# Recurrent branch of a hybrid decoder layer: the gate's sigmoid from exp and tanh instead of a reciprocal, and the low parts of two groups of weights made on VectorE

## The chip, the cores and the metric

The kernel runs on one core of one Trainium2 chip. The metric is the device time of one execution in microseconds (us), lower is better. Engines are named as the profile names them: PE is TensorE (PEld its weight loads), DVE is VectorE, ACT is ScalarE, POOL is GpSimd and SP is SyncE, whose queue issues nearly all transfers.

## The reference

One layer works on 2048 tokens of width 1024 in float32. A normed input goes through one wide projection, whose columns feed three branches: attention with a forgetting bias, a chunked state-space branch (SSD), and a gated linear recurrence over 512 channels. The branch outputs are gated, joined and projected back. The change is in the recurrence:

```
def rglru_mixer(x_raw, conv_w, conv_b, w_a, b_a, w_x, b_x, lam):
    xc = causal_dwconv(x_raw, conv_w, conv_b)
    xb = xc.reshape(bsz, seq, LRU_BLOCKS, LRU_BLOCK_DIM)
    r = sigmoid(einsum('bsnd,nde->bsne', xb, w_a) + b_a)
    i = sigmoid(einsum('bsnd,nde->bsne', xb, w_x) + b_x)
    log_a = -8.0 * r * softplus(-lam)
    a = exp(log_a)
    mult = where(first token, 1.0, sqrt(-expm1(2.0 * log_a)))
    b = mult * (i * xc)
    h[t] = a[t] * h[t-1] + b[t]          # an associative scan
y_lru = rglru_mixer(...) * silu(z_lru)
```

## The kernel before

Each float32 matrix is split into a high and a low part, and a product is three matmuls (high x high, high x low, low x high). `weights` (L172) does this for one group of columns of the input projection: for each of 8 row blocks k it loads `wr` (L184), ACT casts it to the high part `wh` (L186), and an engine that the caller picks (`eng`) subtracts to make the low part `wl` (L187). There are four raw buffers `wr` and nine pairs `wh`, `wl`; so of a new group only row block 0 can be made early, and block k needs the pair that the old group's block k-1 leaves when PE has used it for the last time.

The stages of the program are written one after the other: norm and transposes; the SSD inputs; one group for attention values; then the recurrent stage; then the gate path of the SSD (`zs`, L586 to L597) with the small decay computation `gates`; the SSD units and the attention projections; attention with a first output sweep; and a second output sweep. The order of each engine's queue is set by a scheduler when the program is built, and each engine runs its queue strictly in order.

The recurrent stage (L493 to L582) loops over four blocks m of 128 channels. A block has four pieces of 512 tokens (tb), and each piece three steps, run in the order `LORD`: `x` (projection `pll` on PE, conv on ACT and DVE), `z` (projection `pzl`, gate silu with two POOL multiplications into `ZZ`, L533 to L535), and `g`. On PE a block is 8 projections of 24 matmuls and 4 gate steps of 6, so 216 matmuls. Steps g2 and g3 come last; on ACT, DVE and POOL they run while PE works on the next group, whose weights must be ready by then. Step `g` (L539) computes both gates (`pgal` and `pgxl` in two PSUM buffers), the decay and its square root; after every second piece (one half block, hb, of 1024 tokens) it takes a square root on ACT (L570, with a table load), multiplies (L573), runs the scan on DVE (L574), multiplies into `ZZ` (L578) and stores it to `lr_d` (L579). `ZZ` has one buffer, so the copies L533 of the next half wait until that store has landed, and PE in turn waits for the PSUM that these copies free.

The lines that the change touches in step `g` are, for the recurrence gate r:

```
                pg = gate("a")
                A.activation(ra[:, sl], pg, AF.Exp, scale=-1.0, bias=c1("ba", m))
                V.tensor_scalar(ra[:, sl], ra[:, sl], 1.0, 3.0e38, op0=ALU.add, op1=ALU.min)
                V.reciprocal(ra[:, sl], ra[:, sl])
```

The low parts `wl` of the four recurrent groups and of the first two `zs` groups, 48 in all, are made on POOL; those of all other groups on DVE.

Of the kernel before, what the change touches and what calls it, by code (L numbers as in the profile page):

```python
# [12 lines left out]
AF = mybir.ActivationFunctionType  # L13
ALU = mybir.AluOpType
# [4 lines left out]
P = 128  # L19
# [25 lines left out]
def hybrid_block(ctx, tc, x, norm_g, w_in, q_norm_g, k_norm_g, forget_b, ssd_conv_w, ssd_conv_b,  # L45
# [37 lines left out]
    def ctile(name, shape, dt=F32):  # L83
        return cp.tile(shape, dt, name=name, tag=name)
# [13 lines left out]
    cv = ctile("cv", [P, NV])  # L98
# [4 lines left out]
    dt = ctile("dt", [P, NT, 16])  # L103
    etot = ctile("etot", [P, NT, 16])
    rsn = ctile("rsn", [P, NT, 2])
    lsp = ctile("lsp", [P, 4])
    nlsp = ctile("nlsp", [P, 4])


    def rsqrt(pool, y, v, n, tag):  # L110
# [83 lines left out]
    with tpool(name="p0", bufs=2) as p0, tpool(name="p01", bufs=1) as p01, \  # L194
# [44 lines left out]
        def c1(name, i=0):  # L239
            j = CV[name] + i  # L240
            return cv[:, j:j + 1]
# [24 lines left out]
        for tb in range(4):  # L266
            if tb + AHEAD < 4:
                norm_x(tb + AHEAD)
            for k in range(KD):
                pt, tag = ((psY, "Y"), (pst, "pt"))[(tb * KD + k) % 5 % 2]  # L270
                pt = pt.tile([P, 512], F32, name=f"pu{tb}_{k}", tag=tag)
                for i in range(4):
                    T.transpose(pt[:, i * P:(i + 1) * P],
                                xts[tb * 4 + i][:, k * P:(k + 1) * P], ident)
                g = ngc[:, k:k + 1]
                A.activation(uh[tb][k], pt, AF.Copy, scale=g)
                V.scalar_tensor_tensor(ul[tb][k], pt, g, uh[tb][k].bitcast(F32),
                                       op0=ALU.mult, op1=ALU.subtract)
            if tb == 0:
                pr = psY.tile([P, P], F32, name="pr2", tag="Y")  # L280
                T.transpose(pr, rows, ident)
                V.tensor_copy(cv, pr[:, 0:NV])


                j = CV["cw"]
                V.tensor_scalar(cv[:, j:j + 60], cv[:, j:j + 60], 0.5, None, op0=ALU.mult)
                j = CV["qg"]
                V.tensor_scalar(cv[:, j:j + 1], cv[:, j:j + 1], 0.125, None, op0=ALU.mult)
                j = CV["ba"]
                V.tensor_scalar(cv[:, j:j + 4], cv[:, j:j + 4], -1.0, None, op0=ALU.mult)  # L290
                j = CV["bx"]
                V.tensor_scalar(cv[:, j:j + 4], cv[:, j:j + 4], 0.5, None, op0=ALU.mult)

# [85 lines left out]
    with tpool(name="cvp", bufs=2) as pool, tpool(name="cl", bufs=1) as cl:  # L379
        for gq in range(6):  # L380
            if gq == 3:
                ll = cl.tile([P, 4], F32, name="ll")
                j = CV["lam"]
                V.tensor_scalar(ll, cv[:, j:j + 4], -1.0, None, op0=ALU.mult)
                softplus(cl, lsp, ll, [P, 4], "spl")
                V.tensor_scalar(lsp, lsp, 8.0, None, op0=ALU.mult)
                V.tensor_scalar(nlsp, lsp, -1.0, None, op0=ALU.mult)
            w = weights([(C_X + gq * 256, 256)]) if gq else wx0
            prev = [None, None]
            for tb in range(4):  # L390
                for mm in range(2):
                    m = gq * 2 + mm
                    nm = f"x{m}_{tb}"
                    ps = proj_ch(w, mm, tb, f"px{nm}")
                    acc = pool.tile([P, 512], F32, name=f"acc{nm}", tag="acc")
                    prev[mm] = conv(pool, ps, prev[mm], "cw", "cb", m, nm, 12, acc, str(mm), rtp)
                    th = pool.tile([P, 512], F32, name=f"thx{nm}", tag="thx")
                    A.activation(th, acc, AF.Tanh)
                    V.scalar_tensor_tensor(acc, th, 1.0, acc, op0=ALU.add, op1=ALU.mult)
                    ts = slice(tb * 512, tb * 512 + 512)  # L400
                    if m >= 8:
                        dma((bt_d if m < 10 else ct_d)[m % 2][:, ts], acc)
                    if m < 10:
                        pt = pst.tile([P, 4, P], F32, name=f"ptx{nm}", tag="pt")
                        for i in range(4):
                            T.transpose(pt[:, i, :], acc[:, i * P:(i + 1) * P], ident)
                        st = pool.tile([P, 4, P], F32, name=f"st{nm}", tag="stx")
                        A.copy(st, pt)
                        if m < 8:
                            dst = xs_d[m // 4][ts, (m % 4) * P:(m % 4 + 1) * P]  # L410
                        else:
                            dst = b_d[m - 8][ts, :]
                        dma(dst.rearrange("(i p) c -> p i c", p=P), st)
# [76 lines left out]
    with tpool(name="lxs", bufs=2) as lxs, tpool(name="lp1", bufs=1) as lp1, tpool(name="lp", bufs=2) as pool:  # L490
        wbd = {}
        HB = 1024
        for m in range(4):  # L493
            w = weights([(C_XL + m * P, P), (C_ZL + m * P, P)], eng=G)
            prev = [None]
            for nm, src in (("a", lru_w_a), ("x", lru_w_x)):
                wh = lp1.tile([P, P], F32R, name=f"bdh{nm}{m}", tag=f"bdh{nm}")
# [41 lines left out]
            def stage_g(tb):  # L539
                hb, sl, nm = part(tb)  # L540
                if tb % 2 == 0:
                    RA[hb] = pool.tile([P, HB], F32, name=f"RA{m}_{hb}", tag="RA")
                    MM[hb] = lp1.tile([P, HB], F32, name=f"MM{m}_{hb}", tag="MM")
                xc, ra, mm, zz = XC[hb], RA[hb], MM[hb], ZZ[hb]
                xh, xl = xp.pop(tb)

                def gate(k):
                    wh, wl = wbd[k, m]
                    pg = pst.tile([P, 512], F32, name=f"pg{k}{nm}", tag="pt")
                    T.matmul(pg, wh, xh, start=True, stop=False)  # L550
                    T.matmul(pg, wl, xh, start=False, stop=False)
                    T.matmul(pg, wh, xl, start=False, stop=True)
                    return pg

                pg = gate("a")
                A.activation(ra[:, sl], pg, AF.Exp, scale=-1.0, bias=c1("ba", m))
                V.tensor_scalar(ra[:, sl], ra[:, sl], 1.0, 3.0e38, op0=ALU.add, op1=ALU.min)
                V.reciprocal(ra[:, sl], ra[:, sl])
                pg = gate("x")
                t1 = pool.tile([P, 512], F32, name=f"ti{nm}", tag="t1")  # L560
                A.activation(t1, pg, AF.Tanh, scale=0.5, bias=c1("bx", m))
                V.scalar_tensor_tensor(xc[:, sl], t1, 1.0, xc[:, sl], op0=ALU.add, op1=ALU.mult)
                t2 = pool.tile([P, 512], F32, name=f"tt{nm}", tag="t1")
                A.activation(t2, ra[:, sl], AF.Tanh, scale=lsp[:, m:m + 1])
                A.activation(ra[:, sl], ra[:, sl], AF.Exp, scale=nlsp[:, m:m + 1])
                A.activation(mm[:, sl], ra[:, sl], AF.Square)
                V.scalar_tensor_tensor(mm[:, sl], mm[:, sl], 1.0, t2, op0=ALU.add, op1=ALU.mult)
                if tb % 2 == 0:
                    return
                A.activation(mm, mm, AF.Sqrt)  # L570
                if hb == 0:
                    V.memset(mm[:, 0:1], 1.0)
                V.tensor_tensor(xc, xc, mm, op=ALU.mult)  # L573
                V.tensor_tensor_scan(mm, ra, xc, 0.0 if hcol[0] is None else hcol[0],  # L574
                                     op0=ALU.mult, op1=ALU.add)
                hcol[0] = lp1.tile([P, 1], F32, name=f"hc{m}_{hb}", tag="hc")
                V.tensor_copy(hcol[0], mm[:, HB - 1:HB])
                V.scalar_tensor_tensor(zz, mm, 0.25, zz, op0=ALU.mult, op1=ALU.mult)  # L578
                dma(lr_d[m][:, hb * HB:(hb + 1) * HB], zz)  # L579
# [5 lines left out]
    with tpool(name="zp", bufs=2, side="right") as pool, tpool(name="g1", bufs=1, side="right") as g1:  # L585
        for gq in range(4):  # L586
            if gq == GM:
                gates(g1)
            w = weights([(C_ZS + gq * 256, 256)], eng=G if gq < 2 else V)
            for t2 in range(8):  # L590
                zt = pool.tile([P, 2, 256], F32, name=f"zs{gq}_{t2}", tag="zs")
                ps = proj_tok2(w, t2, f"pzs{gq}_{t2}", (pst, "pt") if t2 % 5 > 2 and gq == 0 else None)
                th = pool.tile([P, 2, 256], F32, name=f"thzs{gq}_{t2}", tag="thzs")
                A.activation(th, ps, AF.Tanh, scale=0.5)
                V.scalar_tensor_tensor(zt, th, 1.0, ps, op0=ALU.add, op1=ALU.mult)
                dst = zs_d[gq // 2][t2 * 256:(t2 + 1) * 256, (gq % 2) * 256:(gq % 2 + 1) * 256]
                dma(dst.rearrange("(i p) c -> p i c", p=P), zt)  # L597
# [455 lines left out]
```

## Time and profile before

| | |
|---|---|
| median of 3 runs | 2083.0 us (2082.02 to 2092.18) |
| profiled execution | 2094.4 us, of which the span from first to last instruction is 2092.4 us |
| PE busy | 2011.2 us, 96% of the span |
| DVE busy | 1278.1 us, 61% |
| ACT busy | 954.3 us, 46% |
| POOL busy | 542.0 us, 26% |
| mean granted TensorE clock | 0.985 of full speed |
| recurrent stage on PE | 376 to 582 us after the start |

The profile is one execution. Where PE is busy without a gap nothing that other engines do shows in the time; so what counts are the gaps of PE, and the stretches in which its clock was granted below full speed.

### The profile page before, as it was taken

What the parts mean: (1) busy time and instruction counts of PE and PEld (TensorE: products, weight loads), DVE (VectorE), ACT (ScalarE), POOL (GpSimd) and SP (SyncE); (2) the same over time, 40 slices, a digit from 0 to 9 for tenths busy, and PEclk for the clock granted to TensorE, in tenths of its full rate; (3) what the DMA queues carried; (4) which work ended last, traced back from release to release, by engine and by line L of the source; (5) the groups of instructions that cost most, each with busy time, mean ns of one, the idle gap of its engine ahead of it and who ended that gap; (6) DMA issues with size and microseconds to landing.
All of it is one profiled execution on the core that took longest, in us unless ns stands there. A gap on an engine that the chain in (4) does not pass through costs nothing. (4 is left out here: it accounts for less than half of the span.)

```text
span 2092.4 us, 38943 instructions
## 1 busy us (share of the span) xinstructions
PE 2011.2 (96%) x14021; PEld 1838.4 (88%) x14021; DVE 1278.1 (61%) x2844; ACT 954.3 (46%) x1985; POOL 542.0 (26%) x750
## 2 busy tenths in 40 slices
PE   7999999999999999998999998999999999998999
PEld 6788888887789998887888996989999999997999
DVE  6654555488874226767576245677787787774333
ACT  8444443466642215454444234566556565652100
POOL 0000001355531004454552001342233323121110
PEclk9999999999999999999999999999999999998999
DMA  5122233111123225666655636365435535234443
GB/s 195 41 71 61 71 112 93 42 42 42 42 72 98 82 80 165 188 182 197 190 166 177 167 116 205 100 165 144 116 110 147 132 105 155 64 100 139 137 133 106
DMA packets 277826, 248.59 MB, mean 119 GB/s; under 512 B 58725, under 2 KB 225153, under 8 KB 275585
## 3 DMA queue, kind: packets, MB, share of 16 engines
q1 hardware_dynamic: 277472, 246.07, 40.6%
q8 instruction: 111, 1.82, 0.4%
q0 software_dynamic: 160, 0.03, 0.1%
q14 instruction: 83, 0.67, 0.1%
HBM read 159.83 MB, written 86.18 MB: 118 GB/s over the span
## 5 line engine op out<-in xcount | busy, mean ns | idle before, releaser
L977 PE MATMUL po<-woh,mh 128*128 128x256 f32 x1024 | 295.2, 289 | 7.3 <-ACT mh L956 7.3
L981 PE MATMUL po<-woh,ml 128*128 128x256 f32 x1024 | 289.3, 283 | 0.0
L979 PE MATMUL po<-wol,mh 128*128 128x256 f32 x1024 | 288.2, 282 | 0.0
L876 ACT CAST ph<-T 128x512 fp32r<-128x512 f32 (+2 forms) x352 | 163.4, 490 | 144.4 <-PE T L869 79.7
L877 DVE TENSOR_TENSOR pl<-T,ph 128x512 fp32r<-128x512 f32 (+2 forms) x352 | 191.0, 563 | 32.5 <-ACT ph L876 32.2
L977 PEld LDWEIGHTS po<-woh,mh 128*128 128x128 f32 x1024 | 193.8, 189 | 10.4 <-ACT mh L956 8.0
L979 PEld LDWEIGHTS po<-wol,mh 128*128 128x128 f32 x1024 | 194.4, 190 | 2.7
L981 PEld LDWEIGHTS po<-woh,ml 128*128 128x128 f32 x1024 | 193.4, 189 | 1.0
L820 ACT ACTIVATE L<-L,mx 128x1920 f32<-128x1920 f32 (+15 forms) x128 | 154.7, 1209 | 54.6 <-DVE mx L819 39.0
L869 PE MATMUL T<-ident,L 128*128 128x128 f32 x1088 | 175.6, 276 | 1.2 <-ACT L L820 0.8
L373 DVE SCALAR_TENSOR_TENSOR accx<-rtx,cv,accx 128x512 f32<-128x512 f32 x144 | 104.6, 752 | 90.4 <-ACT accx L370 76.2
L855 PE MATMUL O<-ph,vv 128*128 128x256 f32 x576 | 154.7, 288 | 3.0 <-ACT ph L876 3.0
L322 PE MATMUL pxx<-uh,wh 128*128 128x512 f32 x384 | 152.7, 400 | 4.7 <-ACT rtx L365 3.3
L856 PE MATMUL O<-pl,vv 128*128 128x256 f32 x576 | 154.1, 291 | 1.0 <-DVE pl L877 0.9
L323 PE MATMUL pxx<-ul,wh 128*128 128x512 f32 x384 | 153.4, 400 | 0.0
L313 PE MATMUL pqk<-wl,uh 128*128 128x256 f32 x512 | 152.6, 299 | 0.8 <-DVE wl L187 0.8
L324 PE MATMUL pxx<-uh,wl 128*128 128x512 f32 x384 | 152.3, 398 | 0.0
L312 PE MATMUL pqk<-wh,uh 128*128 128x256 f32 x512 | 147.8, 293 | 3.0 <-ACT wh L186 3.0
L809 POOL TENSOR_SCALAR_AFFINE_SELECT cm<-cb 128x384 f32<-128x384 f32 (+3 forms) x128 | 58.7, 460 | 352.8 <-DVE mx L816 229.9
L314 PE MATMUL pqk<-wh,ul 128*128 128x256 f32 x512 | 149.5, 294 | 0.0
L313 PE MATMUL pzs<-wl,uh 128*128 128x256 f32 x512 | 144.5, 284 | 3.2 <-POOL wl L187 3.2
L314 PE MATMUL pzs<-wh,ul 128*128 128x256 f32 x512 | 144.4, 283 | 0.0
(313 smaller groups left out, 5661.2 us busy)
## 6 DMA issues: line engine op xcount, KB each, us to landing
ab<-acs_d SPq DMA_DIRECT2D x64, 256.0 KB
wr<-in_w_in_dram SPq DMA_DIRECT2D x192, 64.0 KB
wr<-in_w_in_dram SPq DMA_DIRECT2D x80, 128.0 KB
xt<-in_x_dram SPq DMA_DIRECT2D x16, 512.0 KB
xs_d<-stx SPq DMA_DIRECT2D x32, 256.0 KB
v_d<-vs SPq DMA_DIRECT2D x32, 256.0 KB
zs_d<-zs SPq DMA_DIRECT2D x32, 256.0 KB
xs<-xs_d SPq DMA_DIRECT2D x32, 256.0 KB
```

The source lines that it names most:

```text
L313: T.matmul(ps[:, i, :], h[k][:, sl], wl[k], start=False, stop=False)
L314: T.matmul(ps[:, i, :], l[k][:, sl], wh[k], start=False, stop=(k == KD - 1))
L323: T.matmul(ps, wh[k][:, ms], ul[tb][k], start=False, stop=False)
L820: A.activation(lt[:, 0:n], lt[:, 0:n], AF.Exp, bias=mx, accum_out=sm[:, i:i + 1])
L855: T.matmul(po[:, ca], vv[:, kt, :], ph[:, jj, ca], start=(kt == 0), stop=False)
L856: T.matmul(po[:, ca], vv[:, kt, :], pl[:, jj, ca], start=False, stop=(kt == nk - 1))
L869: ins = T.transpose(pt[:, jj, i * P:(i + 1) * P], L[i][:, kt * P:(kt + 1) * P], ident)
L876: A.copy(ph[:, ja, ca], pt[:, ja, ca])
L877: V.tensor_tensor(pl[:, ja, ca], pt[:, ja, ca], ph[:, ja, ca].bitcast(F32), op=ALU.subtract)
L977: T.matmul(o, mh[:, j, :], h[:, cs], start=(j == 0), stop=False, skip_group_check=True)
L979: T.matmul(o, mh[:, j, :], l[:, cs], start=False, stop=False, skip_group_check=True)
L981: T.matmul(o, ml[:, j, :], h[:, cs], start=False, stop=(j % 4 == 3), skip_group_check=True)
```

## The change

For the recurrence gate, sigmoid(z) = 1/(1 + exp(-z)) is replaced by exp(min(z, 0)) (1 + tanh(|z|/2)) / 2. The factor 2 that is left goes into the constant `lsp` (4 in place of 8). For each of the 16 pieces ACT had one exp and DVE an add with a clamp and a reciprocal; now ACT has a tanh from PSUM and an exp, and DVE a min that reads PSUM, an absolute value and a product. The gate's PSUM buffer is now read by two engines. The 48 low parts that POOL made are made by DVE, since `weights` is called without `eng`. Two more small instructions prepare the constants.

```diff
@@ constants
-    lsp = ctile("lsp", [P, 4])
-    nlsp = ctile("nlsp", [P, 4])
+    lpar = ctile("lpar", [P, 12])
+    lsp, nlsp, bab = (lpar[:, i * 4:i * 4 + 4] for i in range(3))
...
-                V.tensor_scalar(cv[:, j:j + 4], cv[:, j:j + 4], -1.0, None, op0=ALU.mult)
+                V.tensor_copy(bab, cv[:, j:j + 4])
+                V.tensor_scalar(cv[:, j:j + 4], cv[:, j:j + 4], 0.5, None, op0=ALU.mult)
...
-                V.tensor_scalar(lsp, lsp, 8.0, None, op0=ALU.mult)
+                V.tensor_scalar(lsp, lsp, 4.0, None, op0=ALU.mult)
@@ recurrent stage
-            w = weights([(C_XL + m * P, P), (C_ZL + m * P, P)], eng=G)
+            w = weights([(C_XL + m * P, P), (C_ZL + m * P, P)])
...
                 pg = gate("a")
-                A.activation(ra[:, sl], pg, AF.Exp, scale=-1.0, bias=c1("ba", m))
-                V.tensor_scalar(ra[:, sl], ra[:, sl], 1.0, 3.0e38, op0=ALU.add, op1=ALU.min)
-                V.reciprocal(ra[:, sl], ra[:, sl])
+                A.activation(ra[:, sl], pg, AF.Tanh, scale=0.5, bias=c1("ba", m))
+                V.tensor_scalar(mm[:, sl], pg, bab[:, m:m + 1], 0.0, op0=ALU.add, op1=ALU.min)
+                A.activation(mm[:, sl], mm[:, sl], AF.Exp)
+                V.scalar_tensor_tensor(ra[:, sl], ra[:, sl], -1.0, ra[:, sl], op0=ALU.mult,
+                                       op1=ALU.max)
+                V.scalar_tensor_tensor(ra[:, sl], ra[:, sl], 1.0, mm[:, sl], op0=ALU.add,
+                                       op1=ALU.mult)
@@ gate path of the SSD
-            w = weights([(C_ZS + gq * 256, 256)], eng=G if gq < 2 else V)
+            w = weights([(C_ZS + gq * 256, 256)])
```

The queues move with it. The first place is DVE at the end of recurrent block 2 (names: `XC` the conv result, `RA` the gate and decay, `MM` the root and the scan's result, `hc` its last column). Before, from the product ahead of the scan to the first gate step after it:

```order
L573 TENSOR_TENSOR XC_0_4603<-XC_0_4603,MM_0_4708 128x1024
L574 SCALAR_TENSOR_TENSOR MM_0_4708<-RA_0_4707,XC_0_4603 128x1024
L577 COPY hc_0_4818<-MM_0_4708 128x1
L578 SCALAR_TENSOR_TENSOR ZZ_0_4676<-MM_0_4708,ZZ_0_4676 128x1024
L557 TENSOR_SCALAR RA_1_4919<-RA_1_4919 128x512
L558 RECIPROCAL RA_1_4919<-RA_1_4919 128x512
```

The same place on DVE now, where lines after L558 have moved (the scan is L580, the product into `ZZ` L584, the min L559, the absolute value L561):

```order
L579 TENSOR_TENSOR XC_0_4619<-XC_0_4619,MM_0_4724 128x1024
L374 SCALAR_TENSOR_TENSOR XC_1_4746<-rtl_3_4867,cv,XC_1_4746 128x512
L580 SCALAR_TENSOR_TENSOR MM_0_4724<-RA_0_4723,XC_0_4619 128x1024
L187 TENSOR_TENSOR wl_1_4999<-wr_1_4997,wh_1_4998 128x256
L583 COPY hc_0_4838<-MM_0_4724 128x1
L584 SCALAR_TENSOR_TENSOR ZZ_0_4692<-MM_0_4724,ZZ_0_4692 128x1024
L187 TENSOR_TENSOR wl_2_5006<-wr_2_5004,wh_2_5005 128x256
L187 TENSOR_TENSOR wl_3_5013<-wr_3_5011,wh_3_5012 128x256
L187 TENSOR_TENSOR wl_4_5020<-wr_4_5018,wh_4_5019 128x256
L187 TENSOR_TENSOR wl_5_5027<-wr_5_5025,wh_5_5026 128x256
L559 TENSOR_SCALAR MM_1_4940<-pgal_2_4941,lpar 128x512
L561 SCALAR_TENSOR_TENSOR RA_1_4939<-RA_1_4939 128x512
```

A last conv step has come ahead of the scan; the next group's low part 1 stands right behind the scan, parts 2 to 5 behind the product into `ZZ`, and the min that frees the gate's PSUM buffer behind part 5.

The second place is ACT just after that, where the weights of block 3 are cast and gate step g2 of block 2 begins. Before:

```order
L186 CAST wh_5_5002<-wr_5_5001 128x256
L530 ACTIVATE tzl_3_4914<-pzl_3_4889 128x512
L556 ACTIVATE RA_1_4919<-pgal_2_4921,cv 128x512
L533 COPY ZZ_1_4858<-pzl_2_4859 128x512
L533 COPY ZZ_1_4858<-pzl_3_4889 128x512
L186 CAST wh_6_5009<-wr_6_5008 128x256
```

The same place on ACT now:

```order
L186 CAST wh_5_5026<-wr_5_5025 128x256
L531 ACTIVATE tzl_3_4934<-pzl_3_4909 128x512
L534 COPY ZZ_1_4878<-pzl_2_4879 128x512
L534 COPY ZZ_1_4878<-pzl_3_4909 128x512
L558 ACTIVATE RA_1_4939<-pgal_2_4941,cv 128x512
L186 CAST wh_6_5033<-wr_6_5032 128x256
```

The gate's first function has moved behind the two copies into `ZZ`, which wait for the store of `ZZ`.

The third place is the transfer queue SP there, with the loads of the raw weights and that store. Before:

```order
L579 DMA lr_d_103<-ZZ_1_4423 128x1024
L184 DMA wr_5_5001<-in_w_in_dram 128x128 x2
L184 DMA wr_6_5008<-in_w_in_dram 128x128
L579 DMA lr_d_104<-ZZ_0_4676 128x1024
L184 DMA wr_6_5008<-in_w_in_dram 128x128
```

The same place on SP now:

```order
L585 DMA lr_d_103<-ZZ_1_4435 128x1024
L184 DMA wr_5_5025<-in_w_in_dram 128x128 x2
L585 DMA lr_d_104<-ZZ_0_4692 128x1024
L184 DMA wr_6_5032<-in_w_in_dram 128x128 x2
L184 DMA wr_7_5039<-in_w_in_dram 128x128 x2
```

The store has moved ahead of both loads of `wr_6`; those need the raw buffer that low part 2 frees.

## Rows read from the trace of the kernel before

**Rows 1.** The page, part 1: engine, busy us, share of span, instructions.

```profile
PE 2011.2 (96%) x14021; PEld 1838.4 (88%) x14021; DVE 1278.1 (61%) x2844; ACT 954.3 (46%) x1985; POOL 542.0 (26%) x750
```

**Rows 2.** Waits of PE from 320 to 660 us: total us, times, longest.

```profile
PE pvz L299 <- DVE dt L356: 3.8, 1, 3.8
PE pll L324 <- POOL wl L187: 3.2, 4, 1.5
PE pzs L313 <- POOL wl L187: 3.2, 3, 1.9
PE pll L322 <- ACT ZZ L533: 1.4, 2, 0.7
```

**Rows 3.** Windows: length, busy PE, PEld, DVE, ACT, POOL, granted clock, DMA share, GB/s.

```profile
585.00:590.00 5.00, 3.73 (x15) 3.22 (x15) 0.73 (x2) 1.88 (x4) 4.01 (x5) 0.52 0.58 168
590.00:595.00 5.00, 5.00 (x33) 4.71 (x33) 4.93 (x4) 2.42 (x5) 3.93 (x4) 0.80 0.32 94
```

**Rows 4.** Timeline of PE: start us, us, instruction; first matmul of a group.

```profile
425.19 0.39 PE L322 MATMUL pll<-uh,wh 128*128 128x512 f32 x1
...
475.23 0.39 PE L322 MATMUL pll<-uh,wh 128*128 128x512 f32 x1
...
527.92 0.39 PE L322 MATMUL pll<-uh,wh 128*128 128x512 f32 x1
...
581.80 0.28 PE L312 MATMUL pzs<-wh,uh 128*128 128x256 f32 x1
```

**Rows 5.** Timeline of DVE: first scan of each block, and the product into ZZ.

```profile
419.13 3.27 DVE L574 TENSOR_TENSOR_SCAN MM<-RA,XC 128x1024 f32<-128x1024 f32 x1
...
473.01 3.27 DVE L574 TENSOR_TENSOR_SCAN MM<-RA,XC 128x1024 f32<-128x1024 f32 x1
...
526.93 3.27 DVE L574 TENSOR_TENSOR_SCAN MM<-RA,XC 128x1024 f32<-128x1024 f32 x1
...
530.33 1.48 DVE L578 SCALAR_TENSOR_TENSOR ZZ<-MM,ZZ 128x1024 f32<-128x1024 f32 x1
...
580.76 3.27 DVE L574 TENSOR_TENSOR_SCAN MM<-RA,XC 128x1024 f32<-128x1024 f32 x1
```

**Rows 6.** Timelines of POOL, SP and ACT at the end of block 2.

```profile
528.47 6.00 POOL L187 TENSOR_TENSOR wl<-wr,wh 128x256 fp32r<-128x256 f32 x5 [0.42 <-ACT wh L186]
...
532.79 0.42 SPq L579 DMA_DIRECT2D lr_d<-ZZ  x1
...
520.09 0.73 ACT L564 ACTIVATE ttl<-RA,lsp 128x512 f32<-128x512 f32 x1 [3.49 <-DVE RA L558]
...
535.79 1.08 ACT L533 COPY ZZ<-pzl 128x512 f32<-128x512 f32 x2 [1.19 <-DMA lr_d<-ZZ]
```

**Rows 7.** Groups from 325 to 645 us: busy us, mean ns, idle before.

```profile
L558 DVE RECIPROCAL RA<-RA 128x512 f32<-128x512 f32 x16 | 53.7, 3353 | 0.6
...
L565 ACT ACTIVATE RA<-RA,nlsp 128x512 f32<-128x512 f32 x16 | 11.6, 726 | 0.3
...
L556 ACT ACTIVATE RA<-pgal,cv 128x512 f32<-128x512 f32 x16 | 11.0, 689 | 3.0 <-PE pgal L552 3.0
L567 DVE SCALAR_TENSOR_TENSOR MM<-MM,ttl 128x512 f32<-128x512 f32 x16 | 11.0, 686 | 7.3 <-ACT MM L566 7.3
...
L557 DVE TENSOR_SCALAR RA<-RA 128x512 f32<-128x512 f32 x16 | 8.3, 516 | 26.7 <-ACT RA L556 26.7
...
L595 DVE SCALAR_TENSOR_TENSOR zs<-thzs,pzs 128x512 f32<-128x512 f32 x8 | 5.3, 674 | 1.1 <-ACT thzs L594 1.1
```

**Rows 8.** The line of the low parts: ns min/median/max, first and last start.

```profile
L187 DVE TENSOR_TENSOR wl<-wr,wh x128: 408/425/1266, 11.7 to 1231.4; 128x256 fp32r<-128x256 f32 x120, 128x280 fp32r<-128x280 f32 x8
...
L187 POOL TENSOR_TENSOR wl<-wr,wh x48: 727/741/2264, 328.6 to 639.6; 128x256 fp32r<-128x256 f32 x48
```

**Rows 9.** Windows over recurrent block 0 and block 3, columns as in rows 3.

```profile
376.00:425.00 49.00, 49.00 (x215) 39.75 (x215) 26.50 (x29) 23.80 (x40) 20.45 (x21) 1.00 0.14 33
...
528.00:581.00 53.00, 50.06 (x214) 39.41 (x213) 42.75 (x38) 32.95 (x54) 30.18 (x29) 1.00 0.14 41
```

## The prediction

> **What bounds it now.** The page says that PE is busy 96% of the span [rows 1], so I asked first where PE is not busy in the stretch that the change touches. The waits of PE from 320 to 660 us [rows 2] are four: 3.8 us ahead of the recurrent stage, for DVE copies of the group of attention values, which the change does not reach; 3.2 us and 3.2 us for low parts `wl` made on POOL; and 1.4 us for ACT's copies into `ZZ`. Inside block 0 PE has no gap at all (49.00 of 49 us), in the stretch of block 3 it has 50.06 of 53 [rows 9]. So what the change can win is the last three waits, 3.2 + 3.2 + 1.4 = 7.8 us, and what they drag along. That is the clock: after the last of these waits the granted clock reads 0.52 from 585 to 590 us and 0.80 from 590 to 595 [rows 3]. With the low level of 1.2 GHz at half of 2.4, this is 4.8 + 2.0 = 6.8 us at the low level, in which half the work was lost: 3.4 us. Together 11.2 us can come back, 0.54% of the time.
>
> Next, why the low parts are late. The first scan of each block on DVE comes just ahead of the next group's first matmul: scans at 419.13, 473.01, 526.93 and 580.76 [rows 5], first matmuls at 425.19, 475.23, 527.92 and 581.80 [rows 4]. I call the difference the lead: 6.1, 2.2, 1.0 and 1.0 us. With a lead of 6.1 PE waits nowhere. With leads of 1.0 it does: at the end of block 2, POOL makes five low parts in 6.00 us from 528.47 [rows 6], beside that scan and the product behind it. The lead shrinks because DVE is the fullest of the three engines behind PE, 26.50 of 49 us in block 0 and 42.75 of 53 in block 3 [rows 9], and because the last gate step ahead of the scan waits for a reciprocal: ACT idles 3.49 us until it ends [rows 6].
>
> **The sigmoid, part by part.** DVE loses 16 reciprocals of 3.353 us and 16 adds of 0.516 [rows 7], 62.0 us. It gains 16 times three instructions on 128x512: two that read SBUF alone, by the product of the same kind 0.686 each, and a min that reads PSUM, which the trace has no row of; a SBUF form of its shape takes 0.516 and the product that reads PSUM 0.674 [rows 7]. These are its ends; I take 0.674. That is 16 x 2.05 = 32.7 us, so DVE is 29.2 us lighter (31.7 at the lower end). ACT exchanges an exp of 0.689 for a tanh of the same shape and gains 16 exps of 0.726, 11.6 us [rows 7]; in block 3 it is busy 32.95 of 53 [rows 9], so 2.9 more per block fits. Along the path of one gate the old chain is exp 0.69, add 0.52, reciprocal 3.35, together 4.6. The new one is tanh 0.69, the other gate's tanh 0.69 that ACT has next, exp 0.73, product 0.69, together 2.8, with the min and the absolute value beside ACT. The 3.49 us idle goes with it.
>
> **The low parts.** POOL loses 48 instructions, DVE gains 48 x 0.425 = 20.4 us [rows 8]. So DVE is 8.8 us lighter after both edits, 3.8 of it in each recurrent block (4 x 1.82 less minus 8 x 0.425). On POOL one took 0.741 typically and up to 2.264 us [rows 8]. The trace shows what these two engines do to each other: 0.73 us undisturbed on POOL, and 6.00 us for five beside the scan [rows 6, 8]. The Trainium skill, "SBUF — State Buffer", section "SBUF: two separate sides", says why: the two share one pair of ports, which a DVE instruction with two SBUF inputs or a POOL instruction holds to its end while the other is blocked. The trace agrees for the old place of the work; the rule also speaks against the new one, which I take up as a rival.
>
> **What is late next.** On DVE the low parts now stand behind the scan, so I worked out from which lead on PE would not wait. A matmul takes (475.23 - 425.19) / 216 = 0.2317 us [rows 4]. Counted from the scan's start: low part 1 ends at 3.27 + 0.43 = 3.7; the product into `ZZ` takes at most 1.48 [rows 5], so it ends by 5.3 and low part 2 at 5.7. PE needs part 1 after 5 matmuls (1.2 us) and part 2 after 8 (1.9): leads of 2.5 and 3.8 do. The store of `ZZ` took 3.0 us from issue to ACT's copy, 532.79 to 535.79 [rows 6]; it was issued 1.0 us after the product's end, behind a load, and is now ahead of it. It lands at 8.3, the first copy ends by 8.8, and PE needs that PSUM after 18 matmuls, 4.2: a lead of 4.6. Then the second copy, the gate's tanh and the cast of high part 6 end by 10.5, needed after 25 matmuls, 5.8: a lead of 4.7. So 4.7 us is the point.
>
> **The lead that I expect.** Block 0 shows what the steps take without a backlog: 6.1 us. Backlog is what blocks 1 to 3 have more. Of it the gate's chain gives back 1.8 us in each of the steps, DVE's load falls by 3.8 per block, POOL has no low parts ahead of the `ZZ` steps that free ACT's buffers, and the store leaves 1 us earlier. Lost are 0.7 us for the conv step that went ahead of the scan, and ACT's added exps. I expect about 6 us in all blocks, above 4.7 with 1.3 to spare.
>
> **The sum.** 7.8 us of waits and 3.4 us of clock go; nothing replaces them. In the profile's own terms: 2094.4 - 11.2 = 2083.2, a span of 2081.2. Against the median of the runs, 2083.0, which this profiled execution exceeds by 11.4, the same difference gives 2071.8, so 2072 us. The `zs` group changes nothing else: its 8 more low parts, 3.4 us of DVE, stand among the softplus steps of `gates` while PE works on the group before, and each takes 0.425 us where POOL took 0.741 [rows 8]. If that cover fails, PE waits for them, at most the same 3.4 us.
>
> **The rivals.** *The lead stays near 1 us* (20%): the wait moves from POOL's to DVE's low parts. By the same count PE then waits 3.7 - 1.0 - 1.2 = 1.5 for part 1, 5.7 - 1.0 - 1.9 - 1.5 = 1.3 for part 2, about 1 more for the copies: 3.8 per boundary, where it waits 2.6 on the mean (7.8 / 3) now. The clock falls as before: 2083 + 3 x 1.2 = 2087. For it speaks that each low part waits behind a 3.27 us scan; against it, the missing reciprocals.
>
> *Half way* (20%): a lead of 3, 0.8 + 0.9 = 1.7 us left per boundary, the clock kept: 2083 - 7.8 + 5.1 - 3.4 = 2077.
>
> *The shared ports* (10%): the new product and absolute value, and the low parts, read two SBUF inputs, as the instructions did beside which POOL took up to 2.264 instead of 0.727 us [rows 8]. POOL's steps on `ZZ`, on which the next gate's buffers hang, then come about 2 us later (three steps by one 0.69 us instruction each), and some 1 us per boundary reaches PE: 2072 + 3 = 2075. The rule named above is this case; a sum by it alone would be that.
>
> *Slower* (10%): ACT becomes the bound. The gate's PSUM buffer is now freed only when DVE's min has read it, and that stands behind low part 5, while ACT's gate step and the cast of high part 6 stand behind the copies that wait for the store. If this feeds back until the scan starts 2 us after the first matmul, each boundary costs 4.7 + 2 = 6.7: 20.1 against 7.8, and the clock falls at three boundaries instead of one, 6.8 more: 2083 + 12.3 + 6.8 = 2102. It decides from a lead below 4.7 - 2.6 = 2.1 on. ACT's 60% load speaks against it.
>
> **Chances and range.** Forecast 40%, rivals 20, 20, 10 and 10. The range 2066 to 2087 leaves out the last, and a tenth at the other end for a clock that recovers elsewhere too; the forecast's own range is 2068 to 2076. A measurement of this kernel can tell about 0.5%, 10.4 us, from no change: faster is below 2072.6. Most, not all, of the forecast's chance lies there, with little of the others: 0.35. Slower holds the last rival: 0.10. The rest is 0.55.
>
> **What would show it.** In the changed kernel's profile: no wait of PE for `wl` or `ZZ` in the recurrent stage; first scans some 6 us ahead of the next group; a granted clock of 1.00 where `zs` begins; DVE near 39 of 50 us per block. Wrong would be a PE wait for `wl` from DVE, a wait for the gate's PSUM, or a clock that still falls behind block 3.

## The result and the profile after

The changed kernel is slower: a median of 2092.1 us (2087.4 to 2102.7, 22 runs) against 2084.4 us (2077.1 to 2092.2, 22 runs), ratio 1.0042 with a 95% interval of 1.003 to 1.0054, or 7.75 us. 2072 was predicted, with a range up to 2087. One execution of e11 (5041 us, the profiled one) and one of the kernel before beside it (3272 us) lie far outside all others and are left out of every time below.

The profiled execution of the changed kernel has a span of 2088.7 us. The page, part 1, answers to [rows 1]:

```profile
PE 2002.8 (96%) x14021; PEld 1829.1 (88%) x14021; DVE 1273.8 (61%) x2909; ACT 963.3 (46%) x2001; POOL 499.7 (24%) x702
```

DVE is lighter (1278.1 to 1273.8), by 4.3 us where 8.8 was worked out, and POOL is lighter too. It helped nothing. The waits of PE from 320 to 660 us, which answer to [rows 2]:

```profile
PE pll L325 <- DVE wl L187: 4.9, 8, 1.1
PE pll L325 <- DVE hc L583: 3.7, 2, 1.9
PE pvz L300 <- DVE dt L357: 3.6, 1, 3.6
PE pzs L314 <- DVE hc L583: 2.2, 1, 2.2
PE pzs L313 <- ACT ZZ L534: 0.7, 1, 0.7
PE pzs L314 <- DVE wl L187: 0.5, 1, 0.5
PE pll L323 <- ACT ZZ L534: 0.5, 1, 0.5
PE pzs L313 <- ACT wh L186: 0.4, 1, 0.4
```

Without the wait in the group of attention values these are 12.9 us, where there were 7.8. The waits put down to `hc` are waits for low part 1 as well: it stands directly ahead of that small copy in DVE's queue, behind the scan. Next the first scan of each block on DVE, and the first matmul of the group behind block 0 and behind block 3 on PE; they answer to [rows 4, 5]:

```profile
420.09 2.28 DVE L580 TENSOR_TENSOR_SCAN MM<-RA,XC 128x1024 f32<-128x1024 f32 x1
...
424.95 0.39 PE L323 MATMUL pll<-uh,wh 128*128 128x512 f32 x1
...
476.40 2.28 DVE L580 TENSOR_TENSOR_SCAN MM<-RA,XC 128x1024 f32<-128x1024 f32 x1
...
532.65 2.28 DVE L580 TENSOR_TENSOR_SCAN MM<-RA,XC 128x1024 f32<-128x1024 f32 x1
...
588.97 2.28 DVE L580 TENSOR_TENSOR_SCAN MM<-RA,XC 128x1024 f32<-128x1024 f32 x1
...
589.19 0.28 PE L313 MATMUL pzs<-wh,uh 128*128 128x256 f32 x1
```

The scans are 56.31, 56.25 and 56.32 us apart. This is what the reader is to see: the distance is the same each time, so it is a period. In the rows of before [rows 5] it is as regular: 53.88, 53.92, 53.83. PE needs 50.04 us for a block. The lead of 6.1 us in block 0 therefore shrank by 53.88 - 50.04 = 3.84 us in block 1, to 2.2, until PE had to wait for what stands behind the scans. The changed kernel begins with a lead of 4.9, loses it in block 1, and from then on PE runs at the period of the others. From the first matmul behind block 0 to the first of `zs` it takes 589.19 - 424.95 = 164.2 us, before 581.80 - 425.19 = 156.6 [rows 4]: 7.6 us more. The first matmul for `pqk`, the projections behind `zs`, comes at 773.4 us before and at 782.6 now, 9.2 us later; the ratio makes 8.8 us. So the loss lies in this stage and just behind it. Later the two profiled executions, which are one each, differ the other way: that of the kernel before is the longer in all (2094.4 against 2090.6), while its runs spread from 2077 to 2092.

The windows behind block 3, columns as in [rows 3]:

```profile
590.00:595.00 5.00, 2.22 (x8) 1.73 (x9) 4.79 (x7) 1.16 (x5) 2.30 (x1) 0.69 0.17 58
595.00:600.00 5.00, 4.32 (x20) 4.02 (x20) 1.80 (x3) 3.74 (x9) 2.35 (x2) 0.50 0.63 178
600.00:605.00 5.00, 5.00 (x32) 4.72 (x31) 5.00 (x6) 1.79 (x4) 4.94 (x6) 0.78 0.16 31
```

PE is busy for 2.22 of 5 us, and the granted clock falls to 0.50 in the next window, half of 2.4 GHz. It reads 1.00 again from 605 us, after three windows, where it took two before.

**Where the 2.4 us per block come from.** Both traces were walked back from the first scan of a block to that of the block before, for blocks 1 to 3, at each step to what released it, or else to the instruction ahead of it on its engine. The walk meets ACT, DVE and the store of `ZZ`, before the change POOL as well, and never PE. Low parts stand on it in both kernels: before, five on POOL, some 6.3 us in all; now five on DVE, some 5.3 us. It has two halves. From the first scan of a block to its second it is 501.25 - 473.01 = 28.24 us before and 505.85 - 476.40 = 29.45 after; from the second to the next first, 25.68 and 26.80. The timelines of the changed kernel, ACT and DVE by turns, the first two rows from the first half:

```profile
492.10 0.72 ACT L570 ACTIVATE ttl<-RA,lpar 128x512 f32<-128x512 f32 x1 [2.37 <-DVE RA L563]
...
497.92 0.73 ACT L570 ACTIVATE ttl<-RA,lpar 128x512 f32<-128x512 f32 x1 [0.68 <-DVE RA L563]
...
505.85 2.34 DVE L580 TENSOR_TENSOR_SCAN MM<-RA,hc,XC 128x1024 f32<-128x1024 f32 x1
...
513.01 0.59 ACT L534 COPY ZZ<-pzl 128x512 f32<-128x512 f32 x1 [0.73 <-DMA lr_d<-ZZ]
...
515.21 0.81 ACT L371 ACTIVATE XC<-rtl,cv 128x512 f32<-128x512 f32 x1
...
519.91 0.62 ACT L521 CAST xhl<-XC 128x512 fp32r<-128x512 f32 x1 [2.41 <-DVE XC L374]
520.44 0.68 ACT L558 ACTIVATE RA<-pgal,cv 128x512 f32<-128x512 f32 x1
...
522.42 1.79 DVE L568 SCALAR_TENSOR_TENSOR XC<-til,XC 128x512 f32<-128x512 f32 x1
524.13 0.68 DVE L563 SCALAR_TENSOR_TENSOR RA<-RA,MM 128x512 f32<-128x512 f32 x1
...
524.84 0.72 ACT L570 ACTIVATE ttl<-RA,lpar 128x512 f32<-128x512 f32 x1 [2.27 <-DVE RA L563]
...
528.33 1.28 ACT L576 ACT_TABLE_LOAD   x1
...
530.84 1.23 DVE L579 TENSOR_TENSOR XC<-XC,MM 128x1024 f32<-128x1024 f32 x1
531.99 0.75 DVE L374 SCALAR_TENSOR_TENSOR XC<-rtl,cv,XC 128x512 f32<-128x512 f32 x1
```

The same stretch in the timelines of the kernel before, the first three rows from the first half:

```profile
486.16 3.35 DVE L558 RECIPROCAL RA<-RA 128x512 f32<-128x512 f32 x1
...
489.96 0.72 ACT L564 ACTIVATE ttl<-RA,lsp 128x512 f32<-128x512 f32 x1 [1.26 <-POOL ZZ L535]
...
493.62 0.72 ACT L564 ACTIVATE ttl<-RA,lsp 128x512 f32<-128x512 f32 x1
...
501.25 2.35 DVE L574 TENSOR_TENSOR_SCAN MM<-RA,hc,XC 128x1024 f32<-128x1024 f32 x1
...
508.49 0.59 ACT L533 COPY ZZ<-pzl 128x512 f32<-128x512 f32 x1 [4.78 <-DMA lr_d<-ZZ]
508.97 0.82 ACT L370 ACTIVATE XC<-rtl,cv 128x512 f32<-128x512 f32 x1
...
509.41 1.60 DVE L562 SCALAR_TENSOR_TENSOR XC<-til,XC 128x512 f32<-128x512 f32 x1
...
514.32 0.62 ACT L520 CAST xhl<-XC 128x512 fp32r<-128x512 f32 x1 [0.65 <-DVE XC L373]
...
515.33 0.70 ACT L556 ACTIVATE RA<-pgal,cv 128x512 f32<-128x512 f32 x1
...
523.16 1.28 ACT L570 ACT_TABLE_LOAD   x1
...
525.67 1.23 DVE L573 TENSOR_TENSOR XC<-XC,MM 128x1024 f32<-128x1024 f32 x1
```

The first half loses at its second gate. To its first `ttl` it takes 15.70 us instead of 16.95. From there to the second scan it takes 13.75 instead of 11.29, and 2.16 of this lies between the two `ttl`, which come 5.82 us apart instead of 3.66. Before, the second gate's reciprocal had ended at 489.51, while ACT's first `ttl` still waited for POOL's product; so the reciprocal was not on the walk there. Now the second gate's tanh stands on ACT behind all functions of the first gate (494.15), and its min, absolute value and product on DVE come behind that.

In the second half, counted from the scan, the copy into `ZZ` comes at 7.24 before and 7.16 after. Then ACT's conv step of piece 2 went straight on (7.72); now two functions of the gate and the conv's own copy `rtl` stand between (9.36). DVE could take up that conv only at 9.68 before, behind the reciprocal and L562, and takes it up at 10.20 now, with a product of the gate among its steps (516.83). The cast behind the conv comes 1.0 us later (14.06 against 13.07). From that cast to `ttl` [rows 6] the chain took 5.77 and takes 4.93: so much, 0.84 us, is left of the reciprocal's 3.35. From `ttl` to the table load it takes 3.49 instead of 3.07, since functions that need each other now follow each other, 0.76 us from start to start. From the load to the scan it takes 4.32 instead of 3.77: a conv step (L374, 0.66 to the scan's start) has come between the product and the scan. Together 1.0 - 0.84 + 0.42 + 0.55 = 1.13, the difference of the second halves (1.12).

### The profile page after: what moved, and what is told of

Read it like the earlier page. It is cut to its first block, busy times and chain, and to the rows that moved or that the text cites. A ratio compares the mean times of both kernels' runs of the same rounds, so it can differ in the third digit from the quotient of the medians.

```text
span 2088.7 us, 38986 instructions
## 1 busy us (share of the span) xinstructions
PE 2002.8 (96%) x14021; PEld 1829.1 (88%) x14021; DVE 1273.8 (61%) x2909; ACT 963.3 (46%) x2001; POOL 499.7 (24%) x702
## 5 line engine op out<-in xcount | busy, mean ns | idle before, releaser
L374 DVE SCALAR_TENSOR_TENSOR accx<-rtx,cv,accx 128x512 f32<-128x512 f32 x144 | 104.1, 749 | 90.7 <-ACT accx L371 77.0
L862 PE MATMUL O<-pl,vv 128*128 128x256 f32 x576 | 154.1, 291 | 1.0 <-DVE pl L883 0.9
L313 PE MATMUL pzs<-wh,uh 128*128 128x256 f32 x512 | 144.0, 284 | 1.0 <-ACT ZZ L534 0.7
```

What stands on the lines that cost most here:

```text
L313: T.matmul(ps[:, i, :], h[k][:, sl], wh[k], start=(k == 0), stop=False)
L862: T.matmul(po[:, ca], vv[:, kt, :], pl[:, jj, ca], start=False, stop=(kt == nk - 1))
```

## The experiments

Each ratio is to the kernel before, timed beside the run on the same chip. The period is a third of the time from the first scan of block 0 to that of block 3, a mean: in e1, e4, e5, e7, e9, e13 and e14 the three distances differ by 1.0 to 2.3 us, in the others by less than 0.7. Periods and PE times are of one profiled execution each; "PE" is the time from the first matmul behind block 0 to the first of `zs`.

| run | median us | ratio, 95% interval | scans, us | period | PE |
|---|---|---|---|---|---|
| before | 2084.4 | 1 | 419.13, 580.76 | 53.88 | 156.6 |
| changed | 2092.1 | 1.0042 (1.003 to 1.0054) | 420.09, 588.97 | 56.29 | 164.2 |
| e1 | 2087.3 | 1.0022 (1.0011 to 1.0033) | 418.67, 587.20 | 56.18 | 163.5 |
| e2 | 2083.1 | 1.0001 (0.9985 to 1.0018) | 418.52, 584.65 | 55.38 | 160.8 |
| e3 | 2094.9 | 1.0059 (1.0044 to 1.0074) | 421.19, 591.33 | 56.71 | 165.1 |
| e4 | 2096.6 | 1.0057 (1.0039 to 1.0075) | 419.23, 588.24 | 56.34 | 164.3 |
| e5 | 2071.7 | 0.9954 (0.9937 to 0.9971) | 416.08, 569.62 | 51.18 | 150.1 |
| e6 | 2087.3 | 1.0026 (1.001 to 1.0042) | 420.45, 583.70 | 54.42 | 159.5 |
| e7 | 2096.9 | 1.0069 (1.0043 to 1.0096) | 425.63, 595.91 | 56.76 | 165.3 |
| e8 | 2075.4 | 0.9968 (0.9952 to 0.9984) | 414.32, 569.86 | 51.85 | 151.4 |
| e9 | 2083.1 | 0.9996 (0.9979 to 1.0014) | 418.64, 581.69 | 54.35 | 158.1 |
| e10 | 2079.8 | 0.9983 (0.9964 to 1.0002) | 420.45, 580.04 | 53.20 | 154.1 |
| e11 | 2080.8 | 0.9981 (0.9964 to 0.9998) | not read | not read | not read |
| e12 | 2090.5 | 1.0026 (1.0011 to 1.0041) | 417.64, 586.88 | 56.41 | 163.9 |
| e13 | 2085.7 | 1.0016 (0.9999 to 1.0032) | 418.31, 582.88 | 54.86 | 158.7 |
| e14 | 2086.4 | 1.0014 (0.9997 to 1.0031) | 418.68, 582.52 | 54.61 | 159.4 |

**The two parts apart.** e1 takes the changed kernel and gives the low parts back to POOL; e2 takes the kernel before and moves the low parts alone.

```diff
-            w = weights([(C_XL + m * P, P), (C_ZL + m * P, P)])
+            w = weights([(C_XL + m * P, P), (C_ZL + m * P, P)], eng=G)
...
-            w = weights([(C_ZS + gq * 256, 256)])
+            w = weights([(C_ZS + gq * 256, 256)], eng=G if gq < 2 else V)
```

> The changed sigmoid alone; the 48 low parts stay on POOL as before. Theory P (the recurrent stage has a period of its own, set by the chain through ACT, DVE and POOL, 53.9 us per block before and 56.3 after against 50.0 of PE, and the new gate chain made it longer): first scans still some 56 us apart, time 2088 to 2093. Theory Q (the low parts behind the scan on DVE cost it, the sigmoid by itself gains): first scans less than 53.9 us apart, no wait of PE above 1 us for low parts, time 2072 to 2080.

> The low parts alone on DVE; the sigmoid as before, with the reciprocal. Theory P: the period grows only by what stands ahead of the scan or of the product, by 0.5 to 1.5 us from 53.9, time 2084 to 2089. Theory Q: PE waits for low parts behind the scan at each boundary, about 4 us at three of them, and DVE is 5 us fuller per block, time 2092 or more.

The sigmoid alone has the whole period (56.18) and half of the loss, 0.22 of 0.42%; e1 came out 0.7 us below the range of theory P and far above that of Q, by which the sigmoid gains. The low parts alone lengthen the period by 1.5 us and cost nothing measurable; e2 came out 0.9 us below the range of P. In both runs, too, a conv step has come ahead of the scan. Beside the new sigmoid they do cost something at an equal period: PE's waits that the change can reach are 12.9 us in the changed kernel and 10.4 in e1. So Q, which is the first rival of the prediction, may have a part in it.

**Two buffers.** e3 and e4 each give one buffer more.

```diff
-                    MM[hb] = lp1.tile([P, HB], F32, name=f"MM{m}_{hb}", tag="MM")
+                    MM[hb] = pool.tile([P, HB], F32, name=f"MM{m}_{hb}", tag="MM")
```

```diff
-                ZZ[hb] = lp1.tile([P, HB], F32, name=f"ZZ{m}_{hb}", tag="ZZ")
+                ZZ[hb] = pool.tile([P, HB], F32, name=f"ZZ{m}_{hb}", tag="ZZ")
```

> The changed kernel with two buffers for MM (one before), so that the gate's min, which now writes MM at the start of a gate step, need not wait until the product has read the last scan's result. Theory P with this as the cause: the 3.9 us that ACT waits for the min in the middle of a block go, the period falls from 56.3 to about 54 to 55, time 2084 to 2089. Theory Q, or P with only the order of ACT's queue as the cause: the period stays within 0.5 us of 56.3, time 2090 to 2093.

> The changed kernel with two buffers for ZZ, so that ACT's copies need not wait for the store. Theory P: the store (2.6 us from issue to the copy, twice a block) leaves the chain, the period falls to 53 or less, time 2076 to 2084. Theory Q: the low parts now stand behind the product and not only the scan, PE's waits for them stay at 3 us or more per boundary, time 2089 or more.

Both expectations of theory P missed: the periods stayed, 56.71 and 56.34, and the time of e4 is one that theory Q gave. The period of e3 is what was expected if only the order of ACT's queue counts, but its time lies 1.9 us above that range, and why is not known. For `MM` the trace says why: ACT's exp still waits for the min, 3.31 us instead of 3.91, because the min stands behind the scan and the product in DVE's queue, buffer or not. For `ZZ` the copies no longer wait for the store, but the timelines of DVE and POOL show what took its place:

```profile
479.02 6.40 DVE L187 TENSOR_TENSOR wl<-wr,wh 128x256 fp32r<-128x256 f32 x6
...
477.98 2.24 POOL L535 TENSOR_TENSOR tzl<-tzl,ZZ 128x512 f32<-128x512 f32 x1
480.30 1.34 POOL L536 TENSOR_TENSOR ZZ<-tzl,ZZ 128x512 f32<-128x512 f32 x1
481.60 1.46 POOL L535 TENSOR_TENSOR tzl<-tzl,ZZ 128x512 f32<-128x512 f32 x1
483.13 1.33 POOL L536 TENSOR_TENSOR ZZ<-tzl,ZZ 128x512 f32<-128x512 f32 x1
```

POOL's products came up beside six low parts on DVE, which took 1.07 us each.

**The chain cut short, and the order changed.** e5 makes the gate with one tanh, e8 the same with the low parts on POOL. e6 holds the third conv step of pieces 1 and 3 back behind the last scan (`behind`), e7 writes step x of piece 3 earlier.

```diff
                 A.activation(ra[:, sl], pg, AF.Tanh, scale=0.5, bias=c1("ba", m))
-                V.tensor_scalar(mm[:, sl], pg, bab[:, m:m + 1], 0.0, op0=ALU.add, op1=ALU.min)
-                A.activation(mm[:, sl], mm[:, sl], AF.Exp)
-                V.scalar_tensor_tensor(ra[:, sl], ra[:, sl], -1.0, ra[:, sl], op0=ALU.mult,
-                                       op1=ALU.max)
-                V.scalar_tensor_tensor(ra[:, sl], ra[:, sl], 1.0, mm[:, sl], op0=ALU.add,
-                                       op1=ALU.mult)
...
-                A.activation(t2, ra[:, sl], AF.Tanh, scale=lsp[:, m:m + 1])
+                A.activation(t2, ra[:, sl], AF.Tanh, scale=lsp[:, m:m + 1], bias=lsp[:, m:m + 1])
-                A.activation(ra[:, sl], ra[:, sl], AF.Exp, scale=nlsp[:, m:m + 1])
+                A.activation(ra[:, sl], ra[:, sl], AF.Exp, scale=nlsp[:, m:m + 1],
+                             bias=nlsp[:, m:m + 1])
```

```diff
         for k in range(3):
-            V.scalar_tensor_tensor(acc, rt[:, k:k + 512], c1(wname, k * ntile + m), acc,
-                                   op0=ALU.mult, op1=ALU.add)
+            with tc.issue_after(behind.ins) if behind is not None and k == 2 else ExitStack():
+                V.scalar_tensor_tensor(acc, rt[:, k:k + 512], c1(wname, k * ntile + m), acc,
+                                       op0=ALU.mult, op1=ALU.add)
```

```diff
-LORD = "x0 x1 z0 g0 x2 z1 g1 x3 z2 z3 g2 g3"
+LORD = "x0 x1 z0 g0 x2 z1 x3 g1 z2 z3 g2 g3"
```

> The changed kernel with the gate's sigmoid as one tanh on ACT: (1 + tanh(z/2)) / 2, the added one going into the bias of the two functions behind it; no exp, min, absolute value or product. Low parts stay on DVE behind the scan. Theory P (the length of the chain through ACT and DVE sets a period, 56.3 us in the changed kernel): 3 us of chain per half block go, the period falls below 53.9, to about 51, time 2074 to 2082. Theory Q (low parts behind the scan on DVE): their place is as bad as before, PE waits 3 to 4 us per boundary, time 2087 to 2092.

> The changed kernel with the third conv step of pieces 1 and 3 put behind the scan in DVE's queue (ahead of it in the changed kernel). Theory P: each scan comes 0.66 us earlier, the period falls from 56.3 to between 55.0 and 55.7, time 2087 to 2091. Theory Q: low part 1 now stands behind the scan and a conv step, so nothing is gained, time 2092 to 2095.

> The changed kernel with step x of piece 3 written ahead of step g of piece 1. In DVE's queue low parts 1 to 5 of the next group then stand ahead of the scan. Theory P: the chain is as long as before, the period stays at 55 to 57 us, PE loses the same 5 to 6 us per block in other waits, time 2088 or more. Theory Q: PE's waits for low parts vanish and with them the loss, time 2075 to 2083.

> As the tanh-only kernel, with the 48 low parts on POOL. Theory P: the period is that of the tanh-only kernel with low parts on DVE within 1 us, time 2074 to 2082. Theory Q: 4 us or more faster than it.

These four decide between the theories. In e5 the low parts are on DVE as in the changed kernel, and PE loses nothing between the blocks; its time per block is PE's own, 150.1 / 3 = 50.04. The waits of PE from 320 to 660 us in e5:

```profile
PE pvz L300 <- DVE dt L357: 3.4, 1, 3.4
PE pzs L314 <- DVE wl L187: 1.0, 2, 0.8
PE pzs L313 <- ACT wh L186: 0.7, 1, 0.7
PE pgal L551 <- ACT RA L558: 0.3, 1, 0.3
```

It beats both kernels, by 10.3 us against the kernel before timed beside it (2082.1), a little beyond the range expected. e7 put low parts 1 to 5 ahead of the scan, as theory Q would have it, and is no faster than the changed kernel: its period is 56.76, and in place of part of the waits for low parts stand 3.1 us of PE's waits for the gate's PSUM, which the min on DVE has to free. e6 gives back 1.87 us of period with one conv step, more than expected: 4.8 us of PE's time over three blocks, and by the ratios 0.16%, 3.3 us, of the whole, though the intervals of the two ratios overlap. The step's own 0.66 us twice per block is 1.32 us of the period; in the same stretch the product into `ZZ` takes 1.22 us where it took 2.06. The period of e8, 51.85, is within 1 us of that of e5, as expected. Whether e5 is better than e8 the intervals do not say.

**What of the order and what of the work.** e9 is e1, and e10 is e2, with the edit of e6. e11 adds ACT work to the kernel before and no step to the chain; e12 swaps exp and min.

```diff
-                A.activation(ra[:, sl], pg, AF.Exp, scale=-1.0, bias=c1("ba", m))
+                ge = A.activation(ra[:, sl], pg, AF.Exp, scale=-1.0, bias=c1("ba", m))
+                dm = lp1.tile([P, 512], F32, name=f"dm{nm}", tag="dm")
+                with tc.issue_after(ge.ins):
+                    A.activation(dm, ul[0][0].bitcast(F32), AF.Exp)
```

```diff
-                V.tensor_scalar(mm[:, sl], pg, bab[:, m:m + 1], 0.0, op0=ALU.add, op1=ALU.min)
-                A.activation(mm[:, sl], mm[:, sl], AF.Exp)
+                A.activation(mm[:, sl], pg, AF.Exp, bias=bab[:, m:m + 1])
+                V.tensor_scalar(mm[:, sl], mm[:, sl], 1.0, None, op0=ALU.min)
```

> The changed sigmoid alone (low parts on POOL), with the third conv step put behind the scan. Theory P with the conv step's place as the larger part of the added period: the period falls from about 56 to 54.0 to 54.6, time 2082 to 2085, level with the kernel before. If the longer chain through ACT and DVE is the larger part: the period stays at 55.5 or more, time 2086 to 2088.

> The low parts alone on DVE, with the old sigmoid, and the third conv step behind the scan. Theory P: the period falls from 55.4 to 53.9 to 54.7, time 2078 to 2082. Theory Q (the low parts' place behind the scan costs, and now a conv step more stands ahead of them): 2083 to 2087.

> The kernel before with one exp of 128x512 more per gate on ACT, right behind the gate's exp, on data that nothing waits for. It adds the ACT work that the change added (0.73 us, 16 times) and no step to the chain. If ACT's fuller queue lengthens the period: from 53.9 to 55 or more, time 2087 or more. If only the chain's steps and their order count: period 53.9 to 54.4, time 2082 to 2085.

> The changed kernel with exp and min in the other order: exp(min(z,0)) = min(exp(z),1), so ACT makes tanh and exp back to back from PSUM and DVE does all its steps behind them; as many instructions on each engine as in the changed kernel, but the chain no longer goes from ACT to DVE, back and to DVE again. If the crossings between the engines are the cause: the period falls to 54.5 or less, time 2083 to 2087. If the place of the conv step and the order are: the period stays at 55.5 to 56.3, time 2089 to 2093.

The times came out as theory P expects, except that e11 was even a little faster than before; the period of e10, 53.20, fell further than expected. With the conv step behind the scan the new sigmoid is level with the old one (e9), and the low parts on DVE seem to gain 3 to 4 us with the old sigmoid (e10), but its interval just holds 1. ACT's added work by itself costs nothing, and the crossings between the engines do not set the period, which e12 keeps (56.41); its ratio is below that of the changed kernel, but the intervals overlap. e9 and e6 differ in the low parts' engine alone, at periods of 54.35 and 54.42: with the low parts on DVE PE takes 1.4 us more for the three blocks, and the ratio is 1.0026 instead of 0.9996. That is what is left for theory Q: as long as the period makes PE wait for the scan, it also waits for what stands behind it.

**The store once more.** e13 is e1, and e14 is e9, with two buffers for `ZZ`.

> The changed sigmoid alone (low parts on POOL) with two buffers for ZZ. With low parts on DVE the second buffer gained nothing: there the six low parts behind the product took 6.40 us on DVE, beside POOL's products into ZZ that came up from behind the store. If that crowding of DVE and POOL ate the gain: without low parts on DVE the period falls from 56.2 by 1.5 us or more, to 54.7 or less, time 2081 to 2085. If the store was never in the chain that sets the period: it stays at 55.7 or more, time 2086 to 2089.

> As the sigmoid-only kernel with the conv step behind the scan (period 54.35), with two buffers for ZZ as well. If the store is in the chain: the period falls to 53 or less, time 2076 to 2081. If not: 54 to 54.6, time 2082 to 2085.

The two disagree: 1.3 us less period in e13 than in e1, 0.3 more in e14 than in e9, both less than the spread of the single distances there, and no time is gained that the intervals would show. The period of e13 lies between its two expectations, and the time of e14 lies above both of its. So the wait for the store is on the walked chain, but without it other steps are almost as long. Why e14 gained nothing stays open.

## Why the prediction was wrong

**The bound.** The four waits and the clock loss were read rightly, and PE does wait for the engines behind it. What failed is the step "The lead that I expect": it took the shrinking lead for a backlog, which lighter engines would work off, and the 6.1 us of block 0 for what the steps take without one. The scans in [rows 5] already said otherwise: 53.88, 53.92 and 53.83 us apart against PE's 50.04. A lead that falls by period minus PE's time needs a shorter period, and for the forecast it had to fall from 53.9 to about 50. Work taken off an engine that waits in that chain does not do that: DVE became 4.3 us lighter in all, and the period longer.

**The sum of the sigmoid.** The added DVE instructions were taken at 2.05 us per gate. The groups from 325 to 645 us of the changed kernel, columns as in [rows 7]:

```profile
L568 DVE SCALAR_TENSOR_TENSOR XC<-til,XC 128x512 f32<-128x512 f32 x16 | 15.3, 955 | 0.0
L561 DVE SCALAR_TENSOR_TENSOR RA<-RA 128x512 f32<-128x512 f32 x16 | 14.7, 916 | 0.0
L563 DVE SCALAR_TENSOR_TENSOR RA<-RA,MM 128x512 f32<-128x512 f32 x16 | 12.5, 784 | 0.6 <-ACT MM L560 0.3
...
L559 DVE TENSOR_SCALAR MM<-pgal,lpar 128x512 f32<-128x512 f32 x16 | 11.9, 746 | 21.5 <-ACT RA L558 21.5
...
L560 ACT ACTIVATE MM<-MM 128x512 f32<-128x512 f32 x16 | 10.0, 628 | 12.9 <-DVE MM L559 12.9
```

They take 0.75 + 0.92 + 0.78 = 2.45 us. That is a small miss. The large one is the chain's gain, "4.6 to 2.8", 1.8 us per gate: from the gate's first function to `ttl` it is 4.76 before (515.33 to 520.09) and 4.40 after (520.44 to 524.84), 0.36. At the second gate of the first half nothing was to be gained, since its reciprocal was not on the walk, and 2.16 us were lost. In the queue the product for `XC` (L568) stands ahead of the gate's last product, and there takes 1.79 us. The waits in the rows say the rest: DVE 21.5 us for ACT's tanh, ACT 12.9 us for DVE's min.

**The conv step ahead of the scan** was seen, priced at 0.7 us once, and set off against the gains. It comes twice per block; undoing it gave back 4.8 us of PE's time over three blocks (e6), the largest single item, and with low parts on POOL the whole loss of the sigmoid (e1 against e9).

**The low parts.** On DVE, 20.4 us of work were expected and no harm above a lead of 4.7 us. At the lead of 4.9 behind block 0 PE waited 1.0 us; so the count was nearly right, and the lead was not there afterwards.

**The rivals.** The first came nearest: the lead at 0.1 to 0.2 us, and waits of 12.9 / 3 = 4.3 us per boundary where 3.8 were worked out. Its reason, the place behind the scan, is the smaller part (e9 against e6); e5 shows that with a short period the place costs PE next to nothing (1.0 us of waits for low parts), e7 that low parts ahead of the scan do not help while the period stays. The last rival had the sign and the feedback, but not the mechanism: ACT's load is harmless (e11), and PE's wait for DVE's min to free the gate's PSUM appeared only in e7 and e14. The shared ports stand on the walk of the changed kernel: three low parts beside POOL's products take 3.33 us instead of 1.08, and the product L568 takes 1.79 where its median is 0.68. What they add to the time is not shown, since e1, without the low parts on DVE, has the same period.

The measured +0.42% lies inside the 0.5% called no change, which had 0.55; that is luck, since a forecast of -0.5% and rivals of either sign were added up for it and none saw the period.

## What to carry to other kernels

Look at the distance between like events of successive blocks. If it is constant and longer than the busiest engine's work, it is a period and no backlog: walk one period back, and credit a change only with what it takes off that walk, in the order in which the queues will then stand. A long instruction that is replaced by several short ones on two engines that run in order gains what is left after the scheduler has put other work between them; here 0.36 of 3.35 us. The least change that shortens the walk itself, one tanh instead of five instructions, won 10 us.

## What the runs showed of the hardware

Three low parts on DVE with POOL idle, and three beside POOL's products, in the timelines of the changed kernel:

```profile
481.14 1.08 DVE L187 TENSOR_TENSOR wl<-wr,wh 128x256 fp32r<-128x256 f32 x3
...
487.81 3.33 DVE L187 TENSOR_TENSOR wl<-wr,wh 128x256 fp32r<-128x256 f32 x3
...
487.29 3.14 POOL L536 TENSOR_TENSOR ZZ<-tzl,ZZ 128x512 f32<-128x512 f32 x2
```

DVE is slowed threefold, so the blocking that [rows 8] show for POOL holds the other way too. Taken singly, the two POOL products end at 489.01 and 490.43, and a low part 0.28 and 0.29 us after each. The Trainium skill, "SBUF — State Buffer", section "SBUF: two separate sides", says that whichever of the two begins first keeps the shared ports for its whole instruction, where that of DVE reads two inputs from SBUF; the trace agrees.
